# Two input rows in a larger pool of tiles, a lower rank for some splits, and a later time for query blocks, in a layer whose order is planned by the program

## The chip, the cores and the metric

The kernel runs on one core of a Trainium2 chip. The metric is the device time of one launch in microseconds; times of several launches are given by their median. The engines of the core are named as the profile names them: PE (TensorE, matrix products), DVE (VectorE), ACT (ScalarE), POOL (GpSimd) and SP (SyncE, which here only issues DMAs).

## The reference, cut to what matters

One layer with three sub-layers, each normed before and after and added to the residual. `x` is 1024 rows of 1024 float32 values.

```python
h = rmsnorm(x, g_mix_pre)
proj = h @ w_in
y_fox = forgetting_attention(fq, fk, fv, f_logit)       # 8 heads of 64, causal
y_chk = chunked_relpos_attention(cq, ck, cv, rel_bias)  # 8 heads of 64, banded
y = concatenate([rmsnorm(y_fox, g_fox_out), rmsnorm(y_chk, g_chk_out)])
x = x + rmsnorm(y @ w_out, g_mix_post)                  # the mix
h = rmsnorm(x, g_mem_pre)
mem_n = rmsnorm(mem, g_mem_kv)                          # 256 memory rows
q, k, v = h @ w_mq, mem_n @ w_mk, mem_n @ w_mv          # 4 heads of 256
y = softmax(q k^T / 16) v @ w_mo
x = x + rmsnorm(y, g_mem_post)
h = rmsnorm(x, g_ff_pre)
x = x + rmsnorm(square(relu(h @ w_ff1)) @ w_ff2, g_ff_post)   # hidden 4096
```

## The kernel before, in words

Every float32 product is done as three products of split operands: a high part (written by ACT as a copy in a rounded type) and a low part (written by DVE as the difference between the value and its high part). `mm3` (lines 193 to 195) issues high x high, low x high and high x low into one PSUM bank. So each operand of a product costs one ACT and one DVE instruction before PE can use it.

The program has four stages: projections of the first values and norms; an attention phase; a second phase, from the output projection of the mix to the first half of the memory attention's output; and the MLP. The change lies in the second phase. It does, for two halves of 512 rows (`th` 0 and 1):

- `mix_steps`: the products with `w_out` (PSUM tiles `yw`). When the second column half of a block of 128 rows is done, `close_row` (line 1218 on) norms the row block, adds the rows of `x` (tile `xtw`, line 1232), stores the sum to DRAM (`x1d`), squares it (line 1085), and writes the normed block back over `yw` (line 1238). Rows of `x` are loaded by the class `Rows` (line 1212) into tiles `xt`, of which there are two.
- `raw_steps`: the normed blocks are transposed on PE (`tr_h2T`, line 1354), two blocks at a time, and copied by ACT with the gain of the next norm (`h2r`, line 1359). The first half's copies are `raw_q[0, ...]`, the second's `raw_q[1, ...]`.
- `Forms`: the query product `h @ w_mq` is done by seven products of half size instead of eight (Strassen's scheme, Winograd's form). Left operands are three blocks of `h` itself, A11, A12 and A22, and four sums, S1 to S4. `Forms.split` puts the high parts on ACT (line 1432) and then the low parts on DVE (line 1434); `Forms.sums` puts eight additions on DVE, one after the other (line 1415). A22 is the second half's right block, so it waits for the last rows of the mix.
- `query_steps`: PE's seven products (`mq`), in the order A11, A12 (both for two column pairs), A22, S2, S1, S4, S3. `query_final` splits the finished query blocks (`qh` on ACT, line 1462; `ql` on DVE, line 1463) and tells the planner when a block is there (`seen["qm", ...]`).
- `memory_score_steps` (`ms`: the softmax's maximum on DVE, line 1540, its exponent on ACT, line 1542), `memory_turn_steps` (`mtr`) and `memory_out_steps` (`mo`), then a Strassen product with `w_mo` (`ym`).

The order of all this is not written by hand, but planned while the program is built, by the class `Flow`. It holds a clock and, for each of the queues V (DVE), S (ACT), G (POOL) and D (SP's DMA issues), the waiting operations, each with a level, an earliest time, a cost and what follows. When a queue is free in the plan, it takes the waiting operation of the lowest level, and among equals the one that has been ready longest. PE's work comes as streams of steps in order of rank; at each point the first stream whose next step is allowed (its inputs are believed done for 0.2 us, and buffers are free) gives a step. In the second phase the ranks are: memory outputs, memory transposes, memory scores, sums of squares, the row transposes, and last the "filler": mix products, query products, Strassen products. What the plan gives is the fixed order of instructions on each engine. On the chip every engine works through its own list in that order, and waits where an input is not there.

Free buffers are counted as tokens. `free["xt"]` has two, for the row tiles. `free["u4"]` stands for the large pool: one ring of 30 buffers of 4 KB per partition that holds the results of the mix, the raw queries, the forms, the memory's keys and values, operands of the products, and some weights. `Tokens.ready(n)` says that n buffers are free now. At each point pumps run before a step is taken, in this order: weights, rows of `x`, mix outputs, two helpers for sums of weights, forms, and final query blocks.

The levels on ACT in this phase are 0 for softmax exponents, copies out of PSUM, `query_final` and, before the change, all forms; 1 for what `close_row` and the mix's row sums need; 2 for splits of weights.

Of the kernel before, what the change touches and what calls it, by code (L numbers as in the profile page):

```python
# [34 lines left out]
def f(ap):  # L35
    return ap.bitcast(F32)
# [99 lines left out]
def build(ctx, tc, nc, out, t):  # L136
# [16 lines left out]
    def u4(name, shape, dt=F32R):  # L153

        return up.tile(list(shape), dt, tag="u4", bufs=30, name=name)
# [111 lines left out]
    def load_pair(th, p, halves=False):  # L267

        tag = "sp" if th else "klo"
        xt = p1.tile([P, 2, HT], F32, tag=tag, bufs=5 if th else 4, name=f"xT{th}{p}")  # L270
        if not halves:
            nc.sync.dma_start(xt, t["xT"][th, p])
            return xt
        return xt, [lambda j=j: nc.sync.dma_start(xt[:, j, :], t["xT"][th, p][:, j, :]) for j in (0, 1)]
# [68 lines left out]
    def value_leave(g, kb, ps):  # L343
# [12 lines left out]
        if g == 0:  # L356
# [7 lines left out]
    free = {k: Tokens(flow, n) for k, n in  # L364
            dict(s=2, tr=2, pv=2, mm=2, sp=1, p=2, klo=4, bias=2, raw=2, w=0, u4=6,
                 q=4, mp=4, pt=1, xt=2, wq=0, pp=8).items()}
    seen = {}

    def there(*keys):
        return all(flow.past(seen.get(k, math.inf)) for k in keys)  # L370

    def mark(key):
        return lambda at: seen.__setitem__(key, at)
# [25 lines left out]
    class Stock:  # L399
# [81 lines left out]
        def done(self, key):  # L481
            home = self.home.get(key, "w")
            for _ in range(1 + (home in ("u4", "klo"))):
                free[home].give(flow.end)
# [221 lines left out]
    def turn_steps():  # L706
        for n, a, g in units:
            for c, (kbs, slots, dead) in enumerate(key_steps(n, g)):
                yield (0.109 * (4 - len(dead)),
                       lambda: there(("p", n, a, g, 0), ("p", n, a, g, 1)) and free["tr"].ready() and free["p"].ready())  # L710
                free["tr"].take()
                free["p"].take()
                nm = f"{n}{a}{g}{c}"
                live = slice(1 if dead == [0] else 0, 3 if dead == [3] else 4)
                whole = all_of(("t", n, a, g, c), 1)
                tr = mm_tile([P, 4, P], f"ptr{nm}", "tr")
                hl = p1.tile([P, 2, 4, P], F32R, tag="phl", bufs=2, name=f"phl{nm}")
                ph, pl = hl[:, 0], hl[:, 1]
                for m, (j, q) in enumerate(slots):
                    if m not in dead:  # L720
                        sp, b0, i = probs[n, a, g][q]
                        k = kbs[j] - b0
                        nc.tensor.transpose(tr[:, m, :], sp[:, k * P:(k + 1) * P], ident)  # L723

                def split(at, ph=ph, pl=pl, tr=tr, live=live, whole=whole):
                    def done(end):
                        whole(end)
                        free["tr"].give(end)
                    flow.put("V", at, 0.7, lambda: nc.vector.tensor_sub(pl[:, live, :], tr[:, live, :],  # L729
                                                                        f(ph[:, live, :])), done)  # L730

                flow.put("S", flow.end, 0.6, lambda ph=ph, tr=tr, live=live: nc.scalar.activation(  # L732
                    ph[:, live, :], tr[:, live, :], AF.Copy), split)
                trs[n, a, g, c] = hl
            for _ in range(1 + (g > 1)):
                free["sp"].give(flow.end)
# [54 lines left out]
    def all_of(key, m, then=None):  # L791

        count = [m, 0.0]

        def one(at):
            count[0] -= 1
            count[1] = max(count[1], at)
            if count[0] == 0:
                seen[key] = count[1]
                if then:  # L800
                    then(count[1])
        return one
# [199 lines left out]
    gains, ys, h2, h3, xin, outs, qm, pm, pt = {}, {}, {}, {}, {}, {}, {}, {}, {}  # L1002
# [186 lines left out]
    class Rows:  # L1189
# [5 lines left out]
        def pump(self):  # L1195
            while self.left:
                nm, n = self.left[0]
                home = "xt"
                if nm == "w" and n > 5 and not free["xt"].ready() and free["u4"].ready(40):
                    home = "u4"  # L1200
                if not free[home].ready() or nm == "m" and not there(("x1d", n)):
                    break
                self.left.pop(0)
                free[home].take()
                row_home[nm, n] = home

                def load(nm=nm, n=n, home=home):
                    if home == "u4":
                        xin[nm, n] = u4(f"xt{nm}{n}", (P, D), F32)
                    else:  # L1210
                        xin[nm, n] = p2.tile([P, D], F32, tag="xt", bufs=2, name=f"xt{nm}{n}")
                    nc.sync.dma_start(xin[nm, n], t["x"][n * P:(n + 1) * P, :] if nm == "w" else x1d[n])

                flow.load(flow.now, load, mark(("xt", nm, n)))
# [151 lines left out]
    class Forms:  # L1366
# [52 lines left out]
        def split(self, n):  # L1419
            raw = raw_q[n] if n[0] == "S" else raw_q[self.home[n]]  # L1420
            form_q[n] = [u4(f"{n}q_{m}{i}", (P, 2, HT)) for m in "hl" for i in range(2)]
            done = all_of((n + " split",), 2)
            for i in range(2):
                hi, lo = form_q[n][i], form_q[n][i + 2]

                def then(end, i=i):
                    seen["Q", n, i] = end + 0.0
                    done(end)
                    if n in self.spent:
                        self.spent[n](end)  # L1430

                flow.put("S", flow.now, 1.06, lambda hi=hi, r=raw[i]: nc.scalar.activation(hi, r, AF.Copy),
                         lambda at, hi=hi, lo=lo, r=raw[i], then=then: flow.put(
                             "V", at, 1.22, lambda: nc.vector.tensor_sub(lo, r, f(hi)), then, 0), 0)

    class Finals:

# [14 lines left out]
    def query_final(c, th, h, x, at, spent=None):  # L1452
        hi = p2x.tile([P, HT], F32R, tag="qh", bufs=4, name=f"qh{th}{h}{x}")
        lo = p2x.tile([P, HT], F32R, tag="ql", bufs=4, name=f"ql{th}{h}{x}")
        qm[th, h, x] = hi, lo

        def done(end):
            seen["qm", th, h, x] = end
            if spent:
                spent(end)  # L1460

        flow.chain(at, [("S", 0.6, lambda: nc.scalar.activation(hi, c, AF.Copy, scale=0.0625)),
                        ("V", 0.7, lambda: nc.vector.scalar_tensor_tensor(lo, c, 0.0625, f(hi), op0=ALU.mult, op1=ALU.subtract))],
                   done, 0)
# [384 lines left out]
    with tc.manual_schedule():  # L1849
        xt, xloads = load_pair(0, 0, True)  # L1850
# [60 lines left out]
        for kc in range(KC):  # L1911
# [5 lines left out]
            for n in range(3):  # L1917
                for kb in range(4):
                    cs = slice(kb * P, (kb + 1) * P)
                    x = (hT[0].lo if n == 2 else hT[0].hi)(kc, cs)  # L1920
# [133 lines left out]
    def bank(name, tag=None):  # L2054
        if tag is None:
            tag = ("mm", "s", "tr", "pv")[banks[0] % 4]
            banks[0] += 1
        return mm_tile([P, HT], name, tag)
# [84 lines left out]
    def first_row(j, wa, tags=(None, None)):  # L2143

        x = bank(f"px{j}", tags[0])
        product(x, wa, 0, B11)
        yb = bank(f"py{j}", tags[1])
        product(yb, wa, HT, B21)
        p1 = t2(f"p1_{j}")
        nc.scalar.activation(p1, x, AF.Copy)  # L2150
        g11 = t2(f"g11_{j}")
        return x, p1, g11, lambda: nc.vector.tensor_add(g11, yb, p1)
# [324 lines left out]
    with manual:  # L2477
        sums, stores = (lambda: []), []
        for j in range(NP):
            more = j + 1 < NP  # L2480
            after = Weights(j + 2) if j + 2 < NP else None
            w = cur.w
# [10 lines left out]
            if j < AHEAD:  # L2493
                p1, g11 = saved.pop(j)
                x = bank(f"px{j}")
            else:
                x, _, g11, add = first_row(j, w["a"])
# [337 lines left out]
```

## Time and profile before

| | before |
| --- | --- |
| median of 3 runs | 1452.09 us (1449.99 to 1453.26) |
| profiled execution | 1454.28 us |
| its span, first to last instruction | 1452.5 us |
| PE busy | 1436.7 us, 99% of the span |
| DVE, ACT, POOL busy | 78%, 60%, 26% |
| mean granted TensorE clock | 0.996 |
| HBM traffic | 174 GB/s over the span |

A page of the profile gives, for one execution, busy times of the engines, the span in slices, the chain of work that ended last, and the costliest groups of instructions. The trace behind it can be asked for single instructions in order of time, for waits (which engine stood still, and which instruction ended that), and for busy times in any stretch. A row of the timeline gives the start in us from the span's start, the length in us, the engine, the line of the kernel, the operation, output <- inputs, the shapes, and in square brackets how long the engine had stood idle before it and what ended that. "x2" means two such instructions in a row, merged. SPq rows are DMA issues: their length is that of the issue, not of the transfer. Matmuls overlap: a matmul of 128 x 512 is shown with about 0.39 us, while the next one starts some 0.23 us after it. The granted clock is 1.00 at full speed.

### The profile page before, as it was taken

The page shows a single profiled execution, that of the slowest core. Times are in us where ns is not written, and L with a number is a line of the kernel's source. Part 1 is how long each engine was busy: PE and PEld are TensorE (multiplying, and loading weights), DVE is VectorE, ACT ScalarE, POOL GpSimd, SP SyncE. Part 2 cuts the span into 40 slices and gives each one's busy share as a digit, 9 for nine tenths or more (in the row PEclk, how much of TensorE's full clock was granted, in tenths as well). Part 3 has the DMA queues.
Part 4 walks back from the last instruction along what each step waited for, and adds up shares of the span by engine and source line. Part 5 has one row for each costly group of instructions (what it writes and reads, how often), then busy time and mean ns, then how long its engine had stood idle before and what let it go on. Part 6 is the DMA issues. An engine that isn't in the chain of part 4 may idle for free.

```text
span 1452.5 us, 21871 instructions
## 1 busy us (share of the span) xinstructions
PE 1436.7 (99%) x7505; PEld 1224.3 (84%) x7505; DVE 1126.4 (78%) x1918; ACT 871.2 (60%) x1509; POOL 375.0 (26%) x472
## 2 busy tenths in 40 slices
PE   9999999999999999999999999999999999999998
PEld 8988888888888888888888888888888888888886
DVE  6788787867676956778889787896666866789897
ACT  6567676766676845885466555555555555555553
POOL 1145465545554310220113511003323000000003
PEclk9999999999999999999999999999999999999999
DMA  7143423542415586452134646775555996776775
GB/s 277 49 126 92 120 77 131 152 128 57 115 50 147 171 285 209 160 188 88 44 117 161 231 145 229 271 249 183 177 166 189 309 344 245 255 280 232 275 289 203
DMA packets 109439, 262.12 MB, mean 180 GB/s; under 512 B 12280, under 2 KB 30720, under 8 KB 109328
## 3 DMA queue, kind: packets, MB, share of 16 engines
q1 hardware_dynamic: 109184, 260.47, 53.2%
q8 instruction: 59, 0.97, 0.3%
q14 instruction: 52, 0.43, 0.1%
q10 hardware_dynamic: 144, 0.26, 0.0%
HBM read 186.70 MB, written 65.59 MB: 174 GB/s over the span
## 4 chain that ended last, share of the span: by engine, by line
PE 91%; DVE 4%; DMA 2%; ACT 1%; issue 1%; SPq 0%; POOL 0%; DVEq 0%; ACTq 0%; POOLq 0%
PE fx L193 4%; PE fx L194 4%; PE pv L766 4%; PE fx L195 4%; PE ptr L723 4%; PE px L195 3%; PE px L194 3%; PE px L193 3%; PE v L195 2%; PE v L193 2%; PE yw L193 2%; PE q L193 2%; PE v L194 2%; PE yw L194 2%; PE q L194 2%; PE q L195 2%
## 5 line engine op out<-in xcount | busy, mean ns | idle before, releaser
L729 DVE TENSOR_TENSOR phl<-ptr,phl 128x512 fp32r<-128x512 f32 (+1 forms) x152 | 92.3, 615 | 30.9 <-ACT phl L732 29.7
L732 ACT ACTIVATE phl<-ptr 128x512 fp32r<-128x512 f32 (+1 forms) x152 | 79.6, 539 | 49.4 <-PE ptr L723 47.7
L2471 ACT ACTIVATE whif<-ra 128x1024 fp32r<-128x1024 f32 x45 | 47.6, 1058 | 76.9 <-PE fx L194 34.3
L2606 POOL TENSOR_SCALAR rf<-sf 128x1 f32<-128x1 f32 x7 | 6.6, 945 | 313.3 <-ACT jf L2587 313.2
L766 PE MATMUL pv<-phl,vs 128*128 128x512 f32 (+1 forms) x304 | 86.0, 367 | 0.4 <-DVE phl L729 0.4
L2473 DVE TENSOR_TENSOR wlof<-ra,whif 128x1024 fp32r<-128x1024 f32 x45 | 55.0, 1223 | 35.9 <-ACT whif L2471 35.8
L193 PE MATMUL fx<-vhif,whif 128*128 128x512 f32 x168 | 65.6, 390 | 0.0
L194 PE MATMUL fx<-vlof,whif 128*128 128x512 f32 x168 | 65.5, 390 | 0.0
L195 PE MATMUL fx<-vhif,wlof 128*128 128x512 f32 x168 | 65.4, 389 | 0.0
L766 PEld LDWEIGHTS pv<-phl,vs 128*128 128x128 f32 x304 | 54.7, 188 | 10.5 <-DVE phl L729 1.4
L780 POOL TENSOR_TENSOR o<-o 64x256 f32<-64x256 f32 x64 | 47.8, 748 | 51.9 <-DVE o L778 36.1
L2322 POOL TENSOR_TENSOR sc<-wf,wf 128x512 f32<-128x512 f32 x8 | 13.4, 1679 | 177.2 <-DVE s L2135 90.8
L1545 POOL TENSOR_SCALAR mp<-mp,mst 128x256 f32<-128x256 f32 x32 | 22.9, 720 | 127.3 <-DVE mst L1544 104.5
L193 PE MATMUL k<-hT_hi,whik 128*128 128x512 f32 x128 | 53.2, 416 | 0.0
L193 PE MATMUL q<-hT_hi,whiq 128*128 128x512 f32 x128 | 51.8, 404 | 0.0
L778 DVE TENSOR_TENSOR o<-pv,o 64x512 f32<-64x512 f32 x64 | 43.9, 686 | 9.8 <-ACT o L783 8.7
L193 PE MATMUL yw<-whiwo,yT_hi 128*128 128x512 f32 x128 | 50.6, 395 | 0.0
L194 PE MATMUL k<-hT_lo,whik 128*128 128x512 f32 x128 | 50.3, 393 | 0.0
L195 PE MATMUL k<-hT_hi,wlok 128*128 128x512 f32 x128 | 50.3, 393 | 0.0
L194 PE MATMUL yw<-wlowo,yT_hi 128*128 128x512 f32 x128 | 50.2, 392 | 0.0
L195 PE MATMUL q<-hT_hi,wloq 128*128 128x512 f32 x128 | 50.2, 392 | 0.0
L194 PE MATMUL q<-hT_lo,whiq 128*128 128x512 f32 x128 | 50.1, 392 | 0.0
(786 smaller groups left out, 5274.3 us busy)
## 6 DMA issues: line engine op xcount, KB each, us to landing
wg<-in_w_ff SPq DMA_DIRECT2D x48, 512.0 KB, 5.9
ra<-gd SPq DMA_DIRECT2D x40, 512.0 KB, 3.9
wf<-in_w_ff SPq DMA_DIRECT2D x38, 512.0 KB, 3.7
wi<-in_w_ff2q SPq DMA_DIRECT2D x28, 512.0 KB, 6.0
gd<-s SPq DMA_DIRECT2D x32, 256.0 KB, 2.6
gd<-g SPq DMA_DIRECT2D x25, 256.0 KB, 2.9
wrawq<-in_w_qk SPq DMA_DIRECT2D x8, 512.0 KB, 4.3
wrawk<-in_w_qk SPq DMA_DIRECT2D x8, 512.0 KB, 3.6
```

Of the source, the lines that this page charges most:

```text
L193: nc.tensor.matmul(ps, lh, rh, start=start, stop=False, skip_group_check=more)
L194: nc.tensor.matmul(ps, lh, rl, start=False, stop=False, skip_group_check=more)
L195: nc.tensor.matmul(ps, ll, rh, start=False, stop=stop, skip_group_check=more)
L723: nc.tensor.transpose(tr[:, m, :], sp[:, k * P:(k + 1) * P], ident)
L729: flow.put("V", at, 0.7, lambda: nc.vector.tensor_sub(pl[:, live, :], tr[:, live, :], f(ph[:, live, :])), done)
L732: flow.put("S", flow.end, 0.6, lambda ph=ph, tr=tr, live=live: nc.scalar.activation(ph[:, live, :], tr[:, live, :], AF.Copy), split)
L766: nc.tensor.matmul(pv[:, :, qs_, :], v, hl[:, :, hs, :], start=c == 0 and turn == 0, stop=last)
L778: flow.put("V", at, 0.7, lambda: nc.vector.tensor_add(o2[own], pv[own, :, :, ::step], o2[own]), lambda end: (free["pv"].give(end), flow.pu ...
L780: free["pv"].give(end), flow.put("G", end, 0.8, lambda: nc.gpsimd.tensor_add(o2[own, 0], o2[own, 0], o2[own, 1]), store)))
L1545: mul = lambda st=st, pr=pr: nc.gpsimd.tensor_scalar(pr, pr, st[:, 2:3], 1.0, op0=ALU.mult, op1=ALU.mult)
L2471: nc.scalar.activation(ah, ra, AF.Copy)
L2473: nc.vector.tensor_sub(al, ra, f(ah))
```

## The change

There are three edits, all in the second phase. The first: `Rows` may put the rows of `x` for the last two row blocks of the mix (n = 6 and 7) into tiles of the u4 ring when no `xt` tile is free. Before, that was allowed only with 40 free buffers in the ring of 30; now five are enough. The second: in `Forms.split`, the high parts of all forms except A22 go on ACT's queue at level 1 instead of level 0. The low parts stay at level 0 on DVE. The third: `query_final` reports a query block as done 0.3 us later than its planned end, so that the plan allows its memory scores later.

```diff
@@ Rows.pump
                 home = "xt"
-                if nm == "w" and n > 5 and not free["xt"].ready() and free["u4"].ready(40):
+                if nm == "w" and n > 5 and not free["xt"].ready() and free["u4"].ready(5):
                     home = "u4"
@@ Forms.split
                 flow.put("S", flow.now, 1.06, lambda hi=hi, r=raw[i]: nc.scalar.activation(hi, r, AF.Copy),
                          lambda at, hi=hi, lo=lo, r=raw[i], then=then: flow.put(
-                             "V", at, 1.22, lambda: nc.vector.tensor_sub(lo, r, f(hi)), then, 0), 0)
+                             "V", at, 1.22, lambda: nc.vector.tensor_sub(lo, r, f(hi)), then, 0), 0 if n == "A22" else 1)
@@ query_final
         def done(end):
-            seen["qm", th, h, x] = end
+            seen["qm", th, h, x] = end + 0.3
             if spent:
                 spent(end)
```

## The prediction

> **What bounds the kernel now.** I read the page first, for the engine that sets the time; then PE's waits and the busy time by stretches, for where that engine loses time; then the chain in order of time and the timeline, for what ends the loss that the change can reach. From the page:
>
> ```profile
> span 1452.5 us, 21871 instructions
> PE 1436.7 (99%) x7505; PEld 1224.3 (84%) x7505; DVE 1126.4 (78%) x1918; ACT 871.2 (60%) x1509; POOL 375.0 (26%) x472
> ...
> PE 91%; DVE 4%; DMA 2%; ACT 1%; issue 1%; SPq 0%; POOL 0%; DVEq 0%; ACTq 0%; POOLq 0%
> ```
>
> TensorE is busy 1436.7 of 1452.5 us. The change alters no matmul, only the order in which work is queued, so it can move the time only through the 15.8 us in which PE stands still, and through its clock. PE's waits (total, times, longest):
>
> ```profile
> PE sc6g L650 <- DVE mnc6g L654: 2.1, 2, 1.1
> PE ms L193 <- ACT mp L1542: 2.0, 1, 2.0
> ```
>
> The first lies in the attention phase, which the change does not touch. The second, before a memory-score matmul, lies in the second phase, where all three edits are. Busy time by stretches (PE, PEld, DVE, ACT, POOL, then granted clock, DMA share, GB/s):
>
> ```profile
> 450.00:500.00 50.00, 47.56 (x333) 43.39 (x333) 39.91 (x105) 38.63 (x79) 28.02 (x29) 1.00 0.59 174
> ...
> 610.00:620.00 10.00, 10.00 (x46) 8.14 (x45) 9.69 (x14) 9.25 (x16) 3.03 (x3) 1.00 0.19 73
> 620.00:625.00 5.00, 5.00 (x24) 4.11 (x23) 5.00 (x8) 3.45 (x6) 2.77 (x2) 1.00 0.90 338
> 625.00:645.00 20.00, 20.00 (x121) 17.44 (x120) 11.65 (x23) 18.63 (x42) 2.96 (x6) 1.00 0.69 247
> ...
> 645.00:650.00 5.00, 2.97 (x22) 2.67 (x21) 5.00 (x7) 4.60 (x10) 0.00 (x0) 0.99 0.00 0
> 650.00:655.00 5.00, 5.00 (x20) 4.23 (x19) 4.49 (x10) 0.80 (x2) 2.08 (x2) 0.67 0.00 0
> ```
>
> PE loses 5.00 - 2.97 = 2.03 us between 645 and 650, and right behind it the granted clock falls to 0.67 for 5 us: (1 - 0.67) x 5 = 1.7 us more. The stall costs 2.03 + 1.7 = 3.7 us, 0.26% of the span. That is all the change can win in sight. The chain in order of time shows what ends it:
>
> ```profile
> 639.66 0.45 PE tr_h2T L1354 x4
> 640.13 0.84 ACT h2r L1359 x2
> ...
> 641.46 2.19 ACT h2r L1359 x6
> ...
> 644.65 0.95 ACT whimq_T L461
> 645.60 1.89 ACT A22q_h L1432 x2
> ...
> 648.28 0.47 ACT mp L1542 x2
> 648.79 0.39 PE ms L193
> ```
>
> So the last rows of the mix are transposed at 639.66, copied (h2r), and split into the form A22. PE has run out of query products (A22's are next in line), and the score that it could do instead waits for a softmax exponent (mp) that stands on ACT behind A22's two splits. Either would have fed PE: A22 earlier, or the exponent earlier. Why are these rows late? From the timeline, row block 7 (and the loads of blocks 6 and 7):
>
> ```profile
> 605.27 0.38 SPq L446 DMA_DIRECT2D wrawmq_B<-in_w_mq  x1
> ...
> 617.14 1.15 ACT L1238 ACTIVATE yw<-xtw,rw 128x1024 f32<-128x1024 f32 x1
> 618.52 0.38 SPq L1212 DMA_DIRECT2D xtw<-in_x  x1
> 620.31 0.21 DVE L1227 TENSOR_SCALAR rw<-ssw 128x1 f32<-128x1 f32 x1
> 623.88 1.16 ACT L1238 ACTIVATE yw<-xtw,rw 128x1024 f32<-128x1024 f32 x1 [0.96 <-POOL rw L1228]
> 625.06 0.33 SPq L1212 DMA_DIRECT2D xtw<-in_x  x1
> 630.80 1.29 DVE L1232 SCALAR_TENSOR_TENSOR xtw<-yw,rw,xtw 128x1024 f32<-128x1024 f32 x1 [1.81 <-DMA xtw<-in_x]
> 633.84 1.07 ACT L1085 ACTIVATE junk<-xtw 128x1024 bf16<-128x1024 f32 x1
> 637.18 1.15 ACT L1238 ACTIVATE yw<-xtw,rw 128x1024 f32<-128x1024 f32 x1
> ```
>
> There are two xt buffers. The load of block 7 is issued at 625.06, as soon as ACT's L1238 of an earlier block gives one back (623.88 + 1.16), and its addition starts at 630.80, when the load has landed; its own factor (L1227) had been begun at 620.31. The transfer is on the path of the stall.
>
> **The change, part by part.** *First edit, tiles.* The ring u4 has 30 buffers. A threshold of 40 is never met, so before, blocks 6 and 7 always wait for an xt buffer. Counted in the code, the ring has 8 free buffers once the first half's transposes (604.40 below) are queued: 30 less 8 for the memory's keys and values, 2 for weights, 4 + 4 + 4 for the mix's left operand, its result rows and the first half's raw queries. Eight is over 5, so both loads go out there, just behind the weight load of 605.27, instead of 618.52 and 625.06: two issues moved up SP's queue by some 13 and 19 us, none added. The xt buffers that they no longer take go to the loads of the next stage (xtm), which now stand in SP's queue with the same wait for L1238, with the weight loads queued behind as before: I count that nothing.
>
> What it costs: two buffers fewer for the forms.
>
> ```profile
> 604.40 1.91 PE L1354 MATMUL tr_h2T<-ident,yw 128*128 128x128 f32 x16
> 607.90 2.06 ACT L1432 ACTIVATE A11q_h<-h2r 128x1024 fp32r<-128x1024 f32 x2
> 609.80 2.05 ACT L1432 ACTIVATE A12q_h<-h2r 128x1024 fp32r<-128x1024 f32 x2
> 612.53 2.36 DVE L1434 TENSOR_TENSOR A12q_l<-h2r,A12q_h 128x1024 fp32r<-128x1024 f32 x2
> 613.11 0.39 PE L193 MATMUL mq<-A11q_h,whimq_B 128*128 128x512 f32 x1
> 618.85 0.39 PE L194 MATMUL mq<-A12q_l,whimq_B 128*128 128x512 f32 x1
> ```
>
> 8 - 2 - 4 (A11) = 2, and A12 needs 4. It waits until the mix's last product gives back its six, when PE turns to A11's products at 613.11. From there: two high parts by 613.11 + 2.05 = 615.2, the low parts (2.36) behind some 1 us of other DVE work, the first by about 616.5 and the second by 617.7. The first is used at 618.85, the second two steps later: some 2 us of cover, so it costs nothing on the path; without that cover, each us late is a us of PE. In its place ACT and DVE take the squares and gains of blocks 5 to 7 earlier.
>
> *What the rows gain.* Block 7's addition is freed from its transfer: factor and power done, it could start some 6 us before 630.80. But the next two steps are ACT's (L1085, L1238), queued behind level 0 work, and ACT idles only 0.75 + 1.55 + 1.37 = 3.7 us between 610 and 645. That is the most by which the whole ACT order can close up; with the weight split at 644.65 (0.95, lowest level) falling behind A22 it is 4.6 us. At least it is 0. Following ACT's queue by levels I take 3.0, nearer the upper end because the idle stretches lie ahead of these very rows. A22's low parts, and what PE asks for there:
>
> ```profile
> 644.20 0.69 DVE L1463 SCALAR_TENSOR_TENSOR ql<-qv,qh 128x512 fp32r<-128x512 f32 x1 [0.93 <-ACT qh L1462]
> 645.18 0.28 PE L193 MATMUL ms<-km_hi,qh 128*128 128x256 f32 x1
> 647.74 1.22 DVE L1434 TENSOR_TENSOR A22q_l<-h2r,A22q_h 128x1024 fp32r<-128x1024 f32 x1
> 649.21 1.22 DVE L1434 TENSOR_TENSOR A22q_l<-h2r,A22q_h 128x1024 fp32r<-128x1024 f32 x1
> 649.84 0.58 PE L194 MATMUL mq<-A22q_l,whimq_T 128*128 128x512 f32 x1
> 662.55 1.22 DVE L1434 TENSOR_TENSOR S2q_l<-h2r,S2q_h 128x1024 fp32r<-128x1024 f32 x1
> 664.07 0.39 PE L194 MATMUL mq<-S2q_l,whimq_T 128*128 128x512 f32 x1
> ```
>
> Three us earlier they end at 647.74 + 1.22 - 3.0 = 646.0 and 647.4. PE has work until 645.18, or 1.4 us longer where two scores go first. So PE waits 0 to 0.8 us for the first, and 0 to 0.1 for the second, which it needs two steps (1.4 us) later. The ends are 0 and the present 2.03; I take 1.1, a little over the 0.9 of this count, since DVE is busy 5.00 of 5 us there and A22's parts share it with the sums. A wait of 1.1 did not lower the clock in this trace: the two waits of 2.1 us together, longest 1.1, lie in 450 to 500, clock 1.00. So the 1.7 us go as well.
>
> *Second edit, levels.* Six of seven forms lose rank on ACT: 12 splits of about 1.0 us, none added. For A11 and A12 this lets older row work pass (counted above). For S2, S1, S4 and S3 it lets exponents (0.47, the mp row) and copies pass. S2 is tight: its first low part ends at 662.55 + 1.22 = 663.77 and is used at 664.07, 0.3 us later. It hangs on sums that start when the rows have landed (3.0 earlier), while PE comes 2.6 earlier: 0.3 + 3.0 - 2.6 = 0.7 us of cover, less 0.5 for each exponent that passes. The ends are no wait, and 2.3 us if the sums do not move at all; I take 0, as sums and A22 start from the same landing.
>
> *Third edit, 0.3 us.* No instruction is added. Sixteen query blocks (4 heads, 2 blocks, 2 halves) are believed later, so PE places another step ahead of their scores. In the rows above the block's low part ends at 644.89 and its score starts at 645.18, 0.29 later. Where another step is ready this is free, where none is, up to 0.3 each; taken as 0.
>
> *Sum.* 1.1 - 2.03 - 1.7 = -2.6 us. The profiled execution took 1454.28 us (span 1452.5 and 1.8 around it): 1451.7. The median of the runs, 1452.09, stands 2.2 lower: **1449.5 us**.
>
> **The rivals.**
>
> *All of it goes.* A22 arrives 4.6 us earlier, no wait stays: -3.7, 1448.4 us. For it: the idle stretches of ACT; against: the rows' chain is a string of single steps on ACT and DVE, each at the mercy of what is queued at level 0.
>
> *ACT, not the transfer, sets the stall.* ACT is 18.63 of 20 us busy from 625 to 645. If the rows advance by under 1 us, the wait stays near 2 us and the clock falls behind it: 0 to -1, about 1451.5 us.
>
> *The half clock is not this wait's doing*, or is missing from the runs without a profile: then only 2.03 - 1.1 = 0.9 us are won, 1451.2 us. For it: the median stands 2.2 us below the profiled time; against: 0.67 stands directly behind the wait. The Trainium skill, "TensorE: Matmul & The Clock Gate", section "HAM oscillation — how this bites in real kernels", warns of idle gaps over about 3.4 us, and by that rule a gap of 2.03 would not have cost clock speed. This trace differs: the clock falls after 2.03 us.
>
> *Slower: the sums' split behind the softmax.* If S2's high part is held on ACT behind exponents and copies, with 0.3 us of cover PE stops at 664. It breaks even with the 2.6 won at a wait of 0.9 us with a half clock behind it, or 2.6 without. A split that comes 4.5 us late leaves a wait of 4.2, with 1.7 for the clock 5.9: +3.3, 1455.4 us. A12's missing buffers would act likewise at 618.85, past 2 us of cover. For it: ACT and DVE are both full when these splits fall due; against: the sums start earlier too.
>
> **How the numbers follow.** About 0.2% (2.9 us) is what a measurement of this kernel can tell from no change. Forecast 0.34 (1448.5 to 1451); all gone 0.21; ACT sets it 0.13; clock apart 0.12; slower 0.20. Faster by over 0.2% takes the second case and some 0.10 of the forecast, where less wait stays: 0.31. Slower: 0.20. Within: 0.49. The range reaches from 1447.2 (the full gain and 1.2 us of scatter below it; the runs shown spread over 3.3) to 1454.6, which leaves out most of the slower case, whose lighter forms it holds.
>
> **What would show it.** Right: the loads of blocks 6 and 7 stand near 606 on SP; no DVE wait for xtw; A12's splits behind 613; A22's by about 643; the wait before ms L193 gone or under 1.3 us, in its place a short one of mq for A22q_l; clock 1.00 around 650; the span near 1450. Wrong: PE waiting at A12's or S2's first product, A22's splits still after 645, or a new half-clock stretch.

## The result and the profile after

The changed kernel takes 1449.42 us (median of 20 runs, 1448.15 to 1451.88), the kernel before 1452.32 (20 runs): a ratio of 0.9984 with a 95% interval of 0.9977 to 0.9991, so 2.9 us less by the medians, 1.3 to 3.3 by the interval. The page of the kernel after:

```profile
span 1448.0 us, 21869 instructions
...
PE 1436.0 (99%) x7505; PEld 1223.0 (84%) x7505; DVE 1127.7 (78%) x1918; ACT 871.1 (60%) x1509; POOL 373.9 (26%) x472
```

PE does the same 7505 matmuls in the same busy time (1436.7 before). PE's waits after, from 440 to 900 us (total, times, longest):

```profile
PE mq L194 <- DVE A22q_l L1434: 0.4, 1, 0.4
PE mq L194 <- DVE S2q_l L1434: 0.2, 1, 0.2
...
```

The wait of 2.03 us before ms L193 is gone. Two short ones of mq stand in its place. Busy time by stretches (columns as in the prediction): PE is full behind the short wait, and the granted clock stays at 1.00.

```profile
640.00:645.00 5.00, 4.64 (x27) 3.79 (x25) 4.80 (x6) 4.42 (x9) 0.00 (x0) 1.00 0.00 0
645.00:650.00 5.00, 5.00 (x24) 4.19 (x25) 5.00 (x9) 3.01 (x8) 0.00 (x0) 1.00 0.00 0
650.00:655.00 5.00, 5.00 (x31) 4.27 (x30) 4.83 (x11) 3.62 (x8) 4.20 (x3) 1.00 0.02 3
```

The timeline of the kernel after, for the rows that the prediction followed, and for the first products of two stages:

```profile
602.89 0.38 SPq L446 DMA_DIRECT2D wrawmq_B<-in_w_mq  x1
603.36 0.89 SPq L1212 DMA_DIRECT2D xtw<-in_x  x2
...
610.74 0.39 PE L193 MATMUL mq<-A11q_h,whimq_B 128*128 128x512 f32 x1
610.99 1.99 ACT L1432 ACTIVATE A12q_h<-h2r 128x1024 fp32r<-128x1024 f32 x2
613.59 2.35 DVE L1434 TENSOR_TENSOR A12q_l<-h2r,A12q_h 128x1024 fp32r<-128x1024 f32 x2
616.41 0.39 PE L194 MATMUL mq<-A12q_l,whimq_B 128*128 128x512 f32 x1
...
623.36 1.28 DVE L1232 SCALAR_TENSOR_TENSOR xtw<-yw,rw,xtw 128x1024 f32<-128x1024 f32 x1
630.59 0.60 ACT L1507 ACTIVATE qm<-mq 128x512 f32<-128x512 f32 x1 [1.07 <-PE mq L195]
631.08 1.05 ACT L1085 ACTIVATE junk<-xtw 128x1024 bf16<-128x1024 f32 x1
633.64 1.14 ACT L1238 ACTIVATE yw<-xtw,rw 128x1024 f32<-128x1024 f32 x1
641.47 1.99 ACT L1432 ACTIVATE A22q_h<-h2r 128x1024 fp32r<-128x1024 f32 x2
643.68 2.36 DVE L1434 TENSOR_TENSOR A22q_l<-h2r,A22q_h 128x1024 fp32r<-128x1024 f32 x2
644.96 0.50 PE L194 MATMUL mq<-A22q_l,whimq_T 128*128 128x512 f32 x1 [0.36 <-DVE A22q_l L1434]
...
720.05 0.39 PE L193 MATMUL ym<-whimo_B,A11o 128*128 128x512 f32 x1
...
833.01 0.48 PE L193 MATMUL px<-h3T_hi,wah 128*128 128x512 f32 x1
```

And of the kernel before:

```profile
453.55 1.06 ACT L461 ACTIVATE whimk<-wrawmk 128x1024 fp32r<-128x1024 f32 x1 [2.05 <-DMA wrawmk<-in_w_mk]
...
725.13 0.39 PE L193 MATMUL ym<-whimo_B,A11o 128*128 128x512 f32 x1
...
838.07 0.48 PE L193 MATMUL px<-h3T_hi,wah 128*128 128x512 f32 x1
```

Positions of the two traces can't be compared directly, because the stage starts 2.37 us earlier after (610.74 against 613.11, the first product with A11). That part has nothing to do with the change: up to 449.8 us the two traces agree to 0.01 us, then in the execution of before a weight load landed some 2 us later (ACT waits 2.05 us for it at 453.55), and the two waits of 1.0 and 1.1 us that the prediction showed in the attention phase follow. So the measure used below is the time from the first product of mq to the first of ym (mq stage), or on to the first of px (two stages; some experiments move products across the border between them). Before: 725.13 - 613.11 = 112.02 and 838.07 - 613.11 = 224.96 us. After: 109.31 and 222.27. The change wins 2.7 us between these marks. The stage up to the MLP's fx is 0.6 us longer after; no edit touches it, and over the profiles below it scatters by 2.2 us (e11_tiles_late10 left out).

### The profile page after: what moved, and what is told of

Its sections match the earlier page's. It is cut to its first block, busy times and chain, and to the rows that moved or that the text cites. A ratio compares the mean times of both kernels' runs of the same rounds, so it can differ in the third digit from the quotient of the medians.

```text
span 1448.0 us, 21869 instructions
## 1 busy us (share of the span) xinstructions
PE 1436.0 (99%) x7505; PEld 1223.0 (84%) x7505; DVE 1127.7 (78%) x1918; ACT 871.1 (60%) x1509; POOL 373.9 (26%) x472
## 5 line engine op out<-in xcount | busy, mean ns | idle before, releaser
L193 PE MATMUL fx<-vhif,whif 128*128 128x512 f32 x168 | 65.6, 390 | 0.0
L193 PE MATMUL k<-hT_hi,whik 128*128 128x512 f32 x128 | 53.2, 416 | 0.0
L193 PE MATMUL q<-hT_hi,whiq 128*128 128x512 f32 x128 | 51.7, 404 | 0.0
L193 PE MATMUL yw<-whiwo,yT_hi 128*128 128x512 f32 x128 | 50.6, 395 | 0.0
```

The source lines that it names most:

```text
L193: nc.tensor.matmul(ps, lh, rh, start=start, stop=False, skip_group_check=more)
```

## The experiments

All of them start from the kernel before. A loop over a set in `QuerySums.unit` (line 1182) leaves the order of two stores on SP open; here it is fixed, and e0_stores is the control with the other order and no edit. The eight combinations of the three edits come first, then single parts. "Two stages" is the measure above from one profile of each. "Waits" are PE's over 0.25 us in the mq stage, in us. "Ratio" is to the kernel before on the same chip; a median is that of 11 executions, for e7_levels_late of 7 and for e11_tiles_late10 of 4.

| kernel | tiles, levels, 0.3 us | ratio, 95% interval | two stages | waits |
|---|---|---|---|---|
| before | none | 1 | 224.96 | 2.03 (ms) |
| e0_stores | none | 1.0004 [0.9995, 1.0013] | 223.45 | 2.04 (ms) |
| e1_tiles | tiles | 1.0000 [0.9991, 1.0008] | 223.98 | 0.35, 1.31 (mo), 0.31 |
| e2_levels | levels | 1.0026 [1.0018, 1.0035] | 228.21 | 1.19, 3.10 (A22), 0.3 |
| e3_late | 0.3 us | 0.9997 [0.9988, 1.0006] | 223.60 | 2.04 (ms) |
| e5_tiles_levels | tiles, levels | 0.9996 [0.9987, 1.0005] | 223.90 | 0.4, 1.3 (mo), 0.3 |
| e6_tiles_late | tiles, 0.3 us | 1.0008 [0.9999, 1.0017] | 225.31 | 0.4, 0.7, 1.16 (qw) |
| e7_levels_late | levels, 0.3 us | 1.0027 [1.0016, 1.0037] | 227.62 | 1.2, 3.1 (A22) |
| e9_all | all three | 0.9984 [0.9976, 0.9993] | 222.22 | 0.36 |
| e12_s1_level | tiles, S1's level, 0.3 us | 0.9987 [0.9978, 0.9996] | 222.23 | 0.4 |
| e13_one_row | tiles for one row, levels, 0.3 us | 0.9988 [0.9979, 0.9997] | 222.20 | 0.4 |
| e14_a22_first | all three, A22's low parts first | 0.9979 [0.9970, 0.9988] | 221.73 | none |
| e11_tiles_late10 | tiles, 1.0 us | 1.0178 [1.0164, 1.0192] | 245.79 | 0.8 (mo), 0.6, then many |

**Each edit alone.** The edits are those of the diff, one at a time.

```diff
 e1_tiles:   free["u4"].ready(40)  ->  free["u4"].ready(5)
 e2_levels:  then, 0), 0)          ->  then, 0), 0 if n == "A22" else 1)
 e3_late:    = end                 ->  = end + 0.3
 e0_stores:  no edit; the stores of two query sums in the other order
```

> Only the tiles: blocks 6 and 7 may use the large ring with five free buffers; levels and times of query blocks as before. Rows theory (the stall of 2.03 us comes from the last row blocks' late loads, and the tiles alone remove most of it): both loads issued just behind the weight load near 605 us; A22's high parts start by 643; the wait of ms L193 for mp under 1.2 us or gone; no half clock near 650; ratio to before 0.998, that is -2 to -3.5 us. Softmax theory (what counts is who goes first on ACT): A22 no earlier than 645, the wait stays at 2 us, ratio 1.000.

> Only the levels: high parts of all forms but A22 at level 1 on ACT. Rows theory: block 7's addition still waits for its transfer near 630.8 us, A22's high parts start at 645 within 1 us, PE keeps a wait of 1.5 to 2.5 us there with a half clock behind it: ratio 1.000, -0.7 to +0.7 us. Softmax theory: the exponent passes, the wait falls under 1 us, -2 to -3.5 us.

> Only the later query blocks (0.3 us). Rows theory: A22's high parts start at 645 within 1 us and the stall stays, since PE has nothing else to do then: ratio 1.000, -0.7 to +0.7 us. Filler theory (0.3 us makes PE place a product step ahead of scores that are not ready): the wait of ms L193 goes, -2 to -3.5 us.

> Control. Only the order of two neighbouring stores of weight sums (T2 and T4, four pairs in the attention phase) is turned round on SP's queue; that order differs between the two kernels compared, though no line of the change touches it. Every theory of the second phase: ratio 1.000 within 0.0007, the stall of 2 us before ms L193 as before. If these stores set the wait of 2.1 us of sc6g in the attention phase: that wait gone in every execution, -2 us.

The control and the 0.3 us alone can't be told from before. The tiles alone, which were to bring nearly all of the gain, bring nothing: 1.0000. PE's waits of e1_tiles and the rows at the longest of them:

```profile
PE mo L194 <- DVE pl L1572: 1.3, 1, 1.3
PE mq L194 <- DVE A22q_l L1434: 0.4, 1, 0.4
PE mq L195 <- DVE wlomq_T L467: 0.3, 1, 0.3
```

```profile
658.43 2.36 DVE L1434 TENSOR_TENSOR S2q_l<-h2r,S2q_h 128x1024 fp32r<-128x1024 f32 x2
658.53 0.60 ACT L1570 ACTIVATE ph<-mtr 128x512 fp32r<-128x512 f32 x1 [0.20 <-PE mtr L1567]
659.73 0.40 PE L193 MATMUL mo<-ph,vm_hi 128*128 128x512 f32 x1
660.70 0.69 DVE L1572 TENSOR_TENSOR pl<-mtr,ph 128x512 fp32r<-128x512 f32 x1
661.44 0.50 PE L194 MATMUL mo<-pl,vm_hi 128*128 128x512 f32 x1 [1.31 <-DVE pl L1572]
```

The 2.03 us wait is gone, as expected. But the plan now sets the 12 memory output products (mo) straight behind the last product of A22, ahead of all 48 of S2. These products take the transposed softmax results as a high part ph (written by ACT) and a low part pl (written by DVE). pl is queued on DVE behind both low parts of S2 (658.43 to 660.70), though its input ph is there by 659.1. So PE stands still for 1.31 us, and 0.35 + 1.31 + 0.31 = 1.97 us takes the place of 2.03. The stall was moved to the next tight place.

The levels alone make it slower, which neither expectation had. PE's waits of e2_levels:

```profile
PE mq L194 <- DVE A22q_l L1434: 3.1, 1, 3.1
PE mq L193 <- ACT A22q_h L1432: 1.2, 1, 1.2
```

Here block 7's rows are as late as before (load at 622.86 us), but the plan puts nine products of A22 ahead of the scores, so PE has nothing left to do while A22 comes: 4.3 us of waiting where 2.03 were. That the rows stay late was expected rightly, but not that the wait grows.

**Pairs, and lateness of another size.** e9_all, e5_tiles_levels and e6_tiles_late combine the lines above; e11_tiles_late10 has

```diff
 e11_tiles_late10:  ready(40) -> ready(5);   = end  ->  = end + 1.0
```

> All three edits together, with the order of SyncE's stores as in the kernel before, so that nothing but the three edits differs. Theory A (where the mo products stand): block 7's early inputs take away the wait of 2.03 us, and the order of TensorE's products, which puts 9 products of S2 ahead of the 12 of mo, keeps a second wait from coming; ratio to before 0.9975 to 0.9990, waits of the stage below 0.7 us together (about 0.36 for A22q_l, 0.2 for S2q_l). Rival S (the stores' order did it): the gain shrinks to less than 0.05%.

> The tiles and the 0.3 us, the levels as before. Here 24 products of S2 stand ahead of mo, and the value split pl of block 7 ends behind S1q_l on VectorE, by the rows of after at 660.77 + 2.34 = 663.1 us, while mo would start at 658.1 + 24 x 0.23 = 663.7. Theory A: no wait of mo, or one below 0.5 us; ratio 0.9975 to 0.9990 as with all three, so the levels are not needed for it. Rival L (the levels are what the tiles lacked): S2q_h stands ahead of qv and ph on ScalarE as in the kernel with the tiles alone, a wait of about 1.3 us stays, ratio 0.9995 to 1.0005.

> The tiles and the levels, without the 0.3 us. On TensorE and VectorE the order is that of the tiles alone, and on ScalarE one qv stands ahead of the second S2q_h. Theory A: mo still stands ahead of all 48 products of S2 and pl still behind both S2q_l, so mo waits 1.2 to 1.4 us for pl and the ratio is 0.9993 to 1.0007. Rival L: the one swap on ScalarE brings ph and pl forward, the wait of mo falls below 0.5 us, ratio 0.9980 to 0.9990.

> The tiles with 1.0 us of lateness in place of 0.3. The scores of the query blocks stand in runs of 12 as in the kernel after, but mo stands again ahead of all 48 products of S2 and pl behind both S2q_l. Theory A: mo waits 0.8 to 1.8 us for pl, ratio 0.9990 to 1.0005, so the lateness counts only by the place that it gives mo. Rival Q (later query blocks are what helps, by scores in runs of 12): ratio 0.9975 to 0.9988, no wait of mo above 0.5 us.

e9_all repeats the result with the stores' order held. e5_tiles_levels keeps the order of e1_tiles on PE and DVE and keeps its wait of 1.3 us for pl. So what counts is where mo stands, and not the levels by themselves.

e6_tiles_late met neither expectation. mo waits for nothing there, but the time is up, 1.0008. PE's waits:

```profile
PE mq L193 <- DVE qw L1504: 1.2, 1, 1.2
PE mq L195 <- DVE wlomq_T L467: 0.7, 1, 0.7
```

And its timeline:

```profile
658.65 2.00 ACT L1432 ACTIVATE S1q_h<-S1r 128x1024 fp32r<-128x1024 f32 x2
660.27 2.34 DVE L1434 TENSOR_TENSOR S1q_l<-S1r,S1q_h 128x1024 fp32r<-128x1024 f32 x2
660.55 0.59 ACT L1570 ACTIVATE ph<-mtr 128x512 fp32r<-128x512 f32 x1
662.54 0.68 DVE L1572 TENSOR_TENSOR pl<-mtr,ph 128x512 fp32r<-128x512 f32 x1
664.39 0.40 PE L193 MATMUL mo<-ph,vm_hi 128*128 128x512 f32 x1
...
676.28 2.36 DVE L1434 TENSOR_TENSOR S3q_l<-h2r,S3q_h 128x1024 fp32r<-128x1024 f32 x2
678.55 1.22 DVE L467 TENSOR_TENSOR wlomq_B<-wrawmq_B,whimq_B 128x1024 fp32r<-128x1024 f32 x1
679.68 1.28 DVE L1504 TENSOR_TENSOR qw<-mq,qm 128x512 f32<-128x512 f32 x2
680.52 0.47 PE L193 MATMUL mq<-S1q_h,whimq_T 128*128 128x512 f32 x1 [1.16 <-DVE qw L1504]
```

S1's splits go ahead of ph and pl, so mo stands behind 24 products of S2 and starts at 664.39. What follows falls in another order too: on DVE, S3's low parts and a weight split behind them come ahead of the two qw, which take finished results of mq, and PE waits 1.16 us for them. (In e9_all a first qw goes ahead of the weight split, and PE doesn't wait there.) This is not the whole loss: the next stage, ym to px, takes 115.00 us against 112.92 in e9_all. PE's idle time is only 0.4 us more there; part of the rest is products moved across the border, as PE is busy 0.8 us less in the mq stage, and what is left was not followed. The same place with all three edits (e9_all):

```profile
658.61 0.59 ACT L1570 ACTIVATE ph<-mtr 128x512 fp32r<-128x512 f32 x1
659.09 2.01 ACT L1432 ACTIVATE S1q_h<-S1r 128x1024 fp32r<-128x1024 f32 x2
660.23 0.68 DVE L1572 TENSOR_TENSOR pl<-mtr,ph 128x512 fp32r<-128x512 f32 x1
660.83 2.35 DVE L1434 TENSOR_TENSOR S1q_l<-S1r,S1q_h 128x1024 fp32r<-128x1024 f32 x2
660.93 0.39 PE L193 MATMUL mo<-ph,vm_hi 128*128 128x512 f32 x1
```

ph passes S1q_h, pl passes S1q_l, and mo stands behind nine products of S2, just as pl is done.

In e11_tiles_late10 the local expectation held (mo again ahead of S2's products, a wait of 0.78 us for pl, an mq stage of 111.02 us), but the ratio is 1.0178. The loss is in the next stage, 134.78 us in place of 112.96 in the control. Its PE waits from 725 us on begin with

```profile
PE ms L193 <- ACT mp L1542: 5.6, 6, 1.5
PE ym L194 <- DVE wlomo L467: 2.6, 1, 2.6
```

A number that the plan was told, 0.7 us larger, re-sorted the rest of the phase. Why the order came out so badly there was not followed.

**What each of two parts is needed for, and one step further.** One kernel gives only S1's splits the lower rank; one lets only row block 6 into the ring; one puts A22's low parts first on DVE; and one completes the combinations.

```diff
 e12_s1_level:    tiles, 0.3 us, and  then, 0), 1 if n in ("S1",) else 0)
 e13_one_row:     all three, and      n > 5  ->  n == 6
 e14_a22_first:   all three, and the low part's level  0  ->  -1 if n == "A22" else 0
 e7_levels_late:  levels, 0.3 us
```

> The tiles, the 0.3 us and of the levels one split alone: S1's stands behind the softmax, those of A12, S2, S3 and S4 as before. With that one split ScalarE takes ph ahead of S1q_h, VectorE pl ahead of S1q_l, and mo stands behind 9 products of S2 as with all three edits (24 without S1's level). Theory P (the place of ph and so of mo is what the levels give): ratio 0.9976 to 0.9992, waits of the stage below 0.8 us. Rival S (the splits of S2, S3 or S4 must be late for the queues' sake): ratio 1.0000 to 1.0012 as with tiles and 0.3 us alone.

> All three edits, but only row block 6 may take a tile of the big pool; block 7's load waits for an ordinary buffer, freed one block sooner than in the kernel before. The order on TensorE, VectorE, ScalarE and GpSimd is that of all three. Theory P: block 7's load goes out near 617 us, some 8 earlier than in before, lands by its 5.7 us near 622.7, and its add still stands at about 623.4: ratio 0.9976 to 0.9992, no new wait above 0.5 us. Rival E (the loads must go out near 603 us): the add and the sum of squares come 1 to 3 us late, TensorE waits 1 to 2 us, ratio 0.9990 to 1.0003.

> All three edits, and on VectorE the low halves of A22 go ahead of what else is due, so that one of the two S1r sums falls behind them; the scores stand between the products of A22 in other runs (15, 6, 6), and mo behind 6 products of S2. Theory P: the wait of 0.36 us for A22q_l goes, S2q_l's of 0.2 stays, nothing new: ratio 0.9972 to 0.9988, 0 to 0.5 us less than all three. Rival M (any other place of mo brings its wait back): a wait of mo for pl of 0.5 to 1.3 us, ratio 0.9985 to 0.9997.

> The levels and the 0.3 us without the tiles. 12 products of A22 stand ahead of the scores and block 7's load goes out near 623 us as with the levels alone. Theory P: TensorE waits for A22's splits about 1.2 + 3.1 us as with the levels alone, ratio 1.0015 to 1.0035. Rival L (the 0.3 us mends the levels): both waits shrink below 2 us together, ratio 0.9985 to 1.0005.

e12_s1_level does what all three edits do (222.23 against 222.22 us): of the six forms that lose rank, S1 alone is enough. e13_one_row does so too:

```profile
615.78 0.33 SPq L1212 DMA_DIRECT2D xtw<-in_x  x1
...
623.81 1.28 DVE L1232 SCALAR_TENSOR_TENSOR xtw<-yw,rw,xtw 128x1024 f32<-128x1024 f32 x1
```

Block 7's load goes out at 615.78, some 12 us later than after, and its addition starts at 623.81 without a wait (after: 623.36; this trace lies 0.5 us later as a whole). So one borrowed tile is enough; the second wins nothing. e14_a22_first has no wait of PE over 0.25 us left in the stage. Its low parts of A22 stand ahead of the second S1r sum:

```profile
642.72 2.36 DVE L1434 TENSOR_TENSOR A22q_l<-h2r,A22q_h 128x1024 fp32r<-128x1024 f32 x2
645.00 1.22 DVE L1415 TENSOR_TENSOR S1r<-h2r,h2r 128x1024 f32<-128x1024 f32 x1
```

Its two stages take 221.73 us, 0.5 less than all three; 1448.42 us is the lowest median of the study, though its interval overlaps that of e9_all. e7_levels_late has the waits of e2_levels: the levels without the tiles cost some 0.26%, with the 0.3 us or without.

**The half clock.** The control does the same work in the same order as before around the stall and waits 2.04 us there, yet its granted clock behind it is 1.00:

```profile
645.00:650.00 5.00, 2.96 (x21) 2.58 (x21) 5.00 (x7) 3.29 (x9) 0.00 (x0) 1.00 0.00 0
650.00:655.00 5.00, 5.00 (x26) 4.12 (x25) 4.72 (x12) 2.68 (x7) 3.57 (x4) 1.00 0.00 0
```

Its two stages are 224.96 - 223.45 = 1.5 us shorter. e3_late too has the wait and no half clock. The trace's record of the granted clock says why. Each stretch at half speed inside the kernels is 3.413 us long, and the full-speed stretches are whole multiples of that (1440.42 us is 422 of them): the clock is set on a grid of 3.413 us, whose phase differs from execution to execution. Before, the whole wait of 2.03 us lies in one cell (646.5 to 649.9), and the next cell runs at half speed. In e0_stores the edge falls at 646.5, in the middle of the wait: 1.02 us in each cell, no half clock; in e3_late 0.90 and 1.13. Over the 14 profiles, all nine cells with 1.68 us or more of idle PE are followed by half speed; of the cells with 1.53 or less none is (the half speed at each profile's very end left out); of five between, at 1.57 to 1.67, two are. So, while the kernel runs, the limit lies near half a cell, 1.7 us. Two cells at the very end do not fit: after PE's last product they hold 1.93 us (after) and 1.73 us (e14_a22_first) without a product, and full speed follows. Why is open.

The mean clocks of all executions, recorded to three decimals, say how often it happens. On the two chips of e9_all, e12_s1_level, e13_one_row and e14_a22_first, the mean clock of the kernel before is 0.9980 over 56 executions, 21 of them at 0.997 or less; these four kernels, which don't have the wait, show 0.9986 over 44, none of them under 0.998. The difference is 0.9 us for an execution (plus or minus 0.2), about half of the 1.7 us that one stretch at half speed takes off.

The Trainium skill, "TensorE: Matmul & The Clock Gate", section "HAM oscillation — how this bites in real kernels", warns of gaps over some 3.4 us. Here the grid has that step, but a gap of 2.03 us is enough if it falls into one cell.

## Why the prediction was right or wrong

**The sum.** -2.6 us was forecast; the pair of profiles shows -2.7 between the marks, and the medians -2.9 (-2.4 for e9_all). The time is right, but in part by luck: 0.5 us more of the wait went than was counted, and the half clock was worth some 0.7 us less on average (both below). The gain was also put down to the first edit, which alone brings nothing.

**The wait.** 1.1 us were to remain; 0.36 + 0.22 = 0.58 do. The place was right: a short wait of mq for A22q_l in place of the one before ms. But the rows' gain was mis-sized: 3.0 us were counted. A22q_l starts at 643.68 instead of 647.74, 4.06 earlier, of which 2.37 are the stage's earlier start: 1.7 us. Block 7's addition moved by 7.44 (630.80 to 623.36) less 2.37, which is 5.1, but the squares by 2.76 less 2.37, 0.4. In between stands ACT's queue: the sum is ready at 623.36 + 1.28 = 624.6, but its squares start at 631.08, right behind a copy (qm) for which ACT itself had waited 1.07 us. So ACT's queue limits these rows, as the second rival had it, and not the transfer alone. That the wait shrank all the same is due to the plan's order: before, 18 score products stand ahead of A22's first, and the last six of them wait for an exponent; after, 12 stand there.

**The half clock.** Counted as 1.7 us to be won. It costs 1.5 (before against the control), and only where the grid lets it. With an idle time of 2.03 us and a limit near 1.65 (between the bounds above), it falls so in (3.41 - 2.03 + 2 x 0.38) / 3.41 = 63% of positions, an estimate from these numbers: some 0.95 us on average. The recorded clocks above give 0.9, which bears it out. The third rival was half right: the wait causes the half clock, but not in each execution; by the recorded clocks it is not missing from the other executions. Its sign, the profile 2.2 us over the median, is no sign of that: the load that landed late in the attention phase put 2.1 us of waits into this one execution.

With that average, the two stages of the kernel before would take 223.45 + 0.95 = 224.4 us, and the table follows: all three -2.2 (measured -2.4 by the medians), tiles alone -0.4 (0.0), tiles and levels -0.5 (-0.3), tiles and 0.3 us +0.9 (+1.2), levels alone +3.8 (+3.3). All lie within the measured intervals, which reach some 1.2 us to either side.

**First edit, costs.** Right: both loads go out directly behind the weight load; A12's splits stand behind 613 us in before's time (610.99 + 2.37 = 613.4), and the first low part is there some 1.6 us before its use at 616.41 (613.59 + 2.35 / 2 = 614.8). No wait. Wrong: that this edit alone carries the gain. Alone it is worth nothing that can be measured (1.0000, 0.9991 to 1.0008), since the prediction did not ask what PE does after A22: another product that was next in line, mo, took over the stall.

**Second and third edit, counted as 0.** This is the step of the working that failed, though the forecast time came true. Beside the other two, the levels are worth the difference of e6_tiles_late and e9_all, 0.24% or 3.6 us by the medians; the 0.3 us that of e5_tiles_levels and e9_all, 0.12% or 2.0 us. Neither acts by the durations that were counted. The second was costed at S2, the form with 0.3 us of cover, where PE waits 0.2 us with the levels (after) and without (e6_tiles_late); it acts through S1, which gives ph and pl way. The third was costed as 0.3 us at the scores; it acts by the place that the plan gives mo, behind S2's first products instead of ahead of them. The price of an edit that shifts a planned order can't be read from the cost of the shifted instruction.

**The slower rival.** S2 did not stall. But its kind, a split that the plan believes in time and that is late, did happen where the levels stand without the tiles: at A22, 4.3 us, ratio 1.0026. A stage without waits (first rival) was there to be had, by one edit more (e14_a22_first), though its time can't be told from that of e9_all.

## What to carry to other kernels

When a stall is taken away in a tightly packed order, look at the next product in line and at what its operand is queued behind: here the stall of 2.0 us came back as one of 1.3 us some 14 us later and two of 0.3 to 0.4, until two more edits moved the product. Where the order comes from a plan, edits can't be priced one by one: test them together and each without the others, and expect that a number in the plan changed by 0.7 us can cost 25 (e6_tiles_late against e11_tiles_late10). And price a short stall with its clock by several profiles: one execution says only that it can cost the half clock.

## What was not expected of the hardware

The clock's grid of 3.413 us, with a limit near half a cell of idle time in the midst of the kernel, fits with why the same wait cost 1.5 us more in one execution than in another. And the same load in the attention phase, issued within 0.01 us of the same time, landed some 2 us apart in two executions, and put 2.1 us of waits into one of them. Such waits of 1 to 2.1 us in all stand in four of the 14 profiles, with the edits and without.
